# Ten of eleven pairs of the down projection through seven block products, in five groups of two

## The chip, the cores and the metric

The kernel runs on one core of one Trainium2 chip. The metric is the device time of one launch in microseconds (us), the median of several runs. TensorE multiplies matrices into PSUM (8 banks of 128x512 float32), VectorE and ScalarE read PSUM and work on SBUF, SyncE issues the DMAs between the chip's main memory and SBUF. Every instruction of an engine runs in the order in which it was issued to that engine.

## The reference

One encoder layer with a final norm, applied to 1024 + 256 = 1280 tokens of width 1024 (two request groups, the same weights), float32:

```
h = x + 0.5 * swiglu(rmsnorm(x, g1), gate1, up1, down1)
u = rmsnorm(h, gm) @ w_in            # queries, keys, values, retention, gate
h = h + concat(windowed_attention(u), silu(u_gate) * retention(u)) @ w_out
h = h + 0.5 * swiglu(rmsnorm(h, g2), gate2, up2, down2)
y = rmsnorm(h, g_final)
swiglu(x, G, U, D) = (silu(x @ G) * (x @ U)) @ D      # 1024 -> 2816 -> 1024
```

The change lies in the last product, `@ D`, of both feed-forwards.

## The kernel before

Tokens lie along the free dimension, in chunks `CH`: chunks 0 and 1 of 512 tokens, chunk 2 of 256. A tile is 128 features by one chunk. The 2816 inner features are 22 tiles; tile t and tile t + 11 (`HALF` = 11) form pair t, so there are eleven pairs, 0 to 10. Every float32 operand is split into a high and a low fp32r half (`split`, line 517: a cast on ScalarE, a subtraction on VectorE), and every product is three matmuls, high x high, high x low, low x high (`part`, line 535).

A feed-forward (`ffn`, line 663) has two parts. In the first, gate and up, each pair t goes through `product` twice (two "units" of about 25 us); `finish(t)` (line 781) splits its activations and stores them to main memory as tiles `a`. In the second, down, the tiles come back (`act`, line 793, tiles `xa`), and the result `h` (24 tiles: 8 row tiles by 3 chunks) is summed over the pairs.

Down multiplies a 2x2 block matrix (two tiles of a pair by two halves of the 8 row tiles) with a 2x2 block of activations (two tiles of a pair by chunks 0 and 1). `down(ts)` (line 823) does this for the pairs in `ts` with the seven products of Strassen's scheme (Winograd's form): for each of four m, seven products over 512 tokens instead of eight, plus four products for chunk 2's 256 tokens. `seven` (line 628) makes the weight combinations, `combos` (line 618) those of the activations, as operands 6, 7, 5 and 4; operands 1, 2, 3 are tiles as they are, 8 and 9 those of chunk 2. Weights are loaded in two halves `mh`, each for two m. Each finished bank is added into `h` by `add` (line 826): the first addition to a tile is a copy on ScalarE, all later ones are on VectorE. After the second, third and fourth group the residual is loaded and added (lines 898 to 903).

`down_last(ts)` (line 801) does the last two pairs directly, chunk by chunk, so that each chunk is finished in turn and the norm behind it (`after`, a generator) can start: in the first feed-forward `finish1(0)` (line 929), which norms and splits chunk 0 for the input projection, in the second `norm_out` (line 649), which writes the output. Chunk 1's norm in the first feed-forward follows at line 1296, then `factors` (line 919) makes the combinations of both chunks for the products of `joint` (line 1076).

Nothing of this is issued as written. `Weaver` (line 100) records all operations and orders them for each engine by list scheduling with costs and due times (`arrange`, line 269), within the number of buffers: 104 SBUF tiles of 128x512 (`s2`, line 479) are shared by activations, weights, their splits and `h`. A load may be issued up to 300 operations ahead of TensorE's front and must leave 6 tiles free. All DMAs are issued by SyncE in one order. Since all instructions are emitted by one line, every row of the profile bears line 445; groups are told apart by tile names: `pa` and `pb` are PSUM banks (gate/up, and down), `raw` loaded weights, `w`, `wh`, `wl` their halves, `xa` loaded activations, `a` stored ones.

The first group's activations are loaded early, in the last product of gate/up (`early`, line 886).

Of the kernel before, what the change touches and what calls it, by code (L numbers as in the profile page):

```python
# [457 lines left out]
def tile_encoder_layer(ctx: ExitStack, tc: tile.TileContext, xT, wf1, w_in, w_out, wf2,  # L458
# [11 lines left out]
    def nm(s):  # L470
        cnt[0] += 1
        return f"{s}_{cnt[0]}"
# [22 lines left out]
    def bank_b():  # L495
        return nc.tile(psp, [P, 512], F32, "p", nm("pb"), 8, True)
# [7 lines left out]
    cols = nc.tile(cpool, [P, 8], F32, None, "cols", 1)  # L504
# [12 lines left out]
    def split(src, dt_tile_hi, dt_tile_lo):  # L517
        nc.scalar.copy(dt_tile_hi, src)
        nc.vector.tensor_tensor(dt_tile_lo, src, dt_tile_hi.bitcast(F32), op=ALU.subtract)

    def fetch(src, W=512):

        t = big(W, name="raw")
        nc.sync.dma_start(t, src)
        return t

    def halves(t, W=512, together=False):
        hi, lo = two(W, "w", together)
        split(t, hi, lo)
        return hi, lo  # L530

    def unit(src):
        return [halves(fetch(src[:, i * 512:(i + 1) * 512])) for i in range(2)]

    def part(ps, w, x, W, start, stop, cols=None):


        n = 3 * len(x)
        i = 0
        for k, (xh, xl) in enumerate(x):  # L540
            ws = cols if cols is not None else slice(k * P, (k + 1) * P)
            nc.bundle()
            for a, b in ((w[0], xh), (w[0], xl), (w[1], xh)):
                nc.tensor.matmul(ps[:, :W], lhsT=a[:, ws], rhs=b[:, :W], start=start and i == 0,
                                 stop=stop and i == n - 1, skip_group_check=True)
                i += 1
            nc.unbundle()
# [65 lines left out]
    def pair(t, W):  # L613
        a, b = two(W, "x")
        split(t[:, :W], a[:, :W], b[:, :W])
        return a, b

    def combos(b11, b12, b21, b22):


        t1, n2, t3, t4 = (s2(name=n) for n in ("t1", "n2", "t3", "t4"))
        nc.vector.tensor_tensor(t1, b11, b12, op=ALU.subtract)
        nc.vector.scalar_tensor_tensor(n2, t1, -1.0, b22, op0=ALU.mult, op1=ALU.subtract)
        nc.vector.tensor_tensor(t3, b22, b12, op=ALU.subtract)
        nc.vector.scalar_tensor_tensor(t4, n2, -1.0, b21, op0=ALU.mult, op1=ALU.subtract)
        return {i: pair(t, 512) for i, t in ((6, n2), (7, t3), (5, t1), (4, t4))}
# [36 lines left out]
    def ffn(tag, wsrc, leads, factors, load, after, direct_pairs):  # L663
# [4 lines left out]
        HALF = NFF // 2  # L668
# [112 lines left out]
        def finish(t, acts):  # L781
            a11, a12, a21, a22, a1, a2 = acts
            ops = {1: pair(a11, 512), 2: pair(a21, 512), 3: pair(a22, 512),
                   **(combos(a11, a12, a21, a22) if t < HALF - 2 else {10: pair(a12, 512)}),
                   8: pair(a1, 256), 9: pair(a2, 256)}
            for i, p in ops.items():
                keep[t, i] = []
                for n, b in enumerate([p[0].buf] if p[0].buf is p[1].buf else [s.buf for s in p]):
                    d = nc.tile(dp, [P, 512], F32, None, f"a{tag}_{t}_{i}_{n}", 1)
                    nc.sync.dma_start(d, View(b).bitcast(F32))  # L790
                    keep[t, i].append(d)

        def act(t, i):
            out = []
            for d in keep[t, i]:
                s = s2(F32R, "xa")
                nc.sync.dma_start(s.bitcast(F32), d)
                out.append(s)
            return out if len(out) == 2 else (out[0][:, :256], out[0][:, 256:512])

        def down_last(ts, h):
            ws = [unit(wsrc[u, :, 2, :]) for t in ts for u in (t, t + HALF)]
            closing = iter(())
            for c, parts in enumerate(((1, 2), (10, 3), (8, 9))):
                xa = [act(t, i) for t in ts for i in parts]
                W = CH[c][1]
                for d in range(KT):
                    ps = bank_b()
                    for i, (w, x) in enumerate(zip(ws, xa)):
                        part(ps, w[d // 4], [x], W, i == 0, i == len(ws) - 1, slice(d % 4 * P, (d % 4 + 1) * P))  # L810
                    nc.vector.scalar_tensor_tensor(h[c][d][:, :W], ps[:, :W], 0.5, h[c][d][:, :W],
                                                   op0=ALU.mult, op1=ALU.add)

                    if d >= 4:
                        next(closing, None)
                before, closing = closing, iter(after(c))
                next(closing, None)
                for _ in before:
                    pass
            for _ in closing:  # L820
                pass

        def down(ts, h, xa=None):
            xa = xa or {i: [act(t, i) for t in ts] for i in (1, 2, 6, 7, 5, 4, 3, 8, 9)}

            def add(c, d, ps, sign):
                W = CH[c][1]
                if h[c][d] is None:
                    h[c][d] = big(W, name="h")
                    nc.scalar.activation(h[c][d][:, :W], ps[:, :W], AF.Copy, scale=0.5 * sign)  # L830
                else:
                    nc.vector.scalar_tensor_tensor(h[c][d][:, :W], ps[:, :W], 0.5 * sign, h[c][d][:, :W],
                                                   op0=ALU.mult, op1=ALU.add)

            for mh in range(2):
                ws = []
                for t in ts:
                    r = []
                    for u in (t, t + HALF):
                        x = s2(name="raw")  # L840
                        src = wsrc[u, :, 2, :].rearrange("p (i c) -> p i c", i=2)
                        nc.sync.dma_start(x.rearrange("p (i c) -> p i c", i=2), src[:, :, mh * 256:mh * 256 + 256])
                        r.append([x[:, i * 256:i * 256 + 256] for i in range(2)])
                    ws.append(dict(seven(r[0][0], r[1][0], r[0][1], r[1][1], 256)))
                for mm in range(2):
                    m = 2 * mh + mm
                    cols = slice(mm * P, mm * P + P)

                    def all_(ps, i, x, W, start, stop):
                        n = len(ts) - 1  # L850
                        for k, w in enumerate(ws):
                            part(ps, w[i], [xa[x][k]], W, start and k == 0, stop and k == n, cols)

                    X, Y, Z = bank_b(), bank_b(), bank_b()
                    d1, d2 = bank_b(), bank_b()
                    all_(X, 1, 1, 512, True, True)
                    add(0, m, X, 1)
                    all_(d1, 1, 8, 256, True, False)
                    all_(Z, 2, 2, 512, True, True)
                    add(0, m, Z, 1)  # L860
                    all_(d1, 2, 9, 256, False, True)
                    add(2, m, d1, 1)
                    all_(X, 6, 6, 512, False, True)
                    add(0, m + 4, X, -1)
                    all_(Y, 7, 7, 512, True, True)
                    add(1, m + 4, Y, -1)
                    all_(X, 5, 5, 512, False, True)
                    add(1, m + 4, X, -1)
                    all_(Y, 4, 4, 512, False, True)
                    add(0, m + 4, Y, -1)  # L870
                    all_(d2, 4, 9, 256, True, False)
                    all_(X, 3, 3, 512, False, True)
                    add(1, m, X, 1)
                    all_(d2, 21, 8, 256, False, True)
                    add(2, m + 4, d2, 1)

        last = next(leads)
        finish(0, direct(0, last))
# [5 lines left out]
        first = {}  # L884

        def early(i):
            if i == 2:
                first.update({j: [act(0, j)] for j in (1, 2, 6, 7, 5, 4, 3, 8, 9)})

        for t in range(direct_pairs, HALF):  # L890
            finish(t, seven_eighths(t, t == direct_pairs, *[early] * (t == HALF - 1)))
        for c in range(3):
            h[c] = [None] * KT
        groups = [[0], [1, 2], [3, 4], [5, 6], [7, 8]]
        for n, g in enumerate(groups):
            down(g, h, first if n == 0 else None)

            if 1 <= n <= 3:
                c = n - 1
                W = CH[c][1]  # L900
                for d in range(KT):
                    t = load(c, d)
                    nc.vector.tensor_tensor(h[c][d][:, :W], h[c][d][:, :W], t[:, :W], op=ALU.add)
        down_last([9, 10], h)


    h = {c: [None] * KT for c in range(3)}
# [386 lines left out]
    for c in pr:  # L1294
        if c == 1:
            finish1(1)
        ps = [bank_a(), bank_a()]
# [22 lines left out]
    for name, ld, col in (("wf", LDF, 0), ("wb", LDB, 1), ("cf", LDF, 4), ("cb", LDB, 4)):  # L1320
        t = nc.tile(cpool, [P, 4], F32, None, name, 1)
# [177 lines left out]
```

## Time and profile before

| | |
|---|---|
| runs | 2270.89, 2273.5, 2271.23 us; median 2271.23 |
| profiled execution | 2270.64 us, of which the span from first to last instruction 2268.7 |
| mean granted clock of TensorE | 0.995 of 2.4 GHz |
| busy: TensorE | 2236.5 us (99%) |
| busy: VectorE | 1646.5 us (73%) |
| busy: ScalarE | 982.7 us (43%) |
| moved by DMA | 340.06 MB, mean 150 GB/s |

A record of a matmul is longer than its share of the engine, because matmuls overlap; what the engine spends on one is the distance between starts. The number of matmuls is that of the instructions of TensorE. A wait is put down to the instruction that came last before it ended.

### The profile page before, as it was taken

What the parts mean: (1) busy time and instruction counts of PE and PEld (TensorE: products, weight loads), DVE (VectorE), ACT (ScalarE), POOL (GpSimd) and SP (SyncE); (2) the same over time, 40 slices, a digit from 0 to 9 for tenths busy, and PEclk for the clock granted to TensorE, in tenths of its full rate; (3) what the DMA queues carried; (4) which work ended last, traced back from release to release, by engine and by line L of the source; (5) the groups of instructions that cost most, each with busy time, mean ns of one, the idle gap of its engine ahead of it and who ended that gap; (6) DMA issues with size and microseconds to landing.
All of it is one profiled execution on the core that took longest, in us unless ns stands there. A gap on an engine that the chain in (4) does not pass through costs nothing.

```text
span 2268.7 us, 34074 instructions
## 1 busy us (share of the span) xinstructions
PE 2236.5 (99%) x12234; PEld 1916.9 (84%) x12234; DVE 1646.5 (73%) x3259; ACT 982.7 (43%) x2058; POOL 27.7 (1%) x31
## 2 busy tenths in 40 slices
PE   9999999999999999999999999999999999999998
PEld 8788888888888888888788778888888888888887
DVE  8966666665778769986888886586656666487856
ACT  7533444334422235344788574354433444432311
POOL 0000000000000000000000100000000000000000
PEclk9999999999999999999999999999999999999999
DMA  4333343335776633335533353143333334857722
GB/s 169 126 116 128 137 158 108 121 112 192 277 247 231 216 114 98 116 103 173 186 103 93 128 180 107 50 160 130 112 116 112 130 131 145 281 200 267 254 74 93
DMA packets 198601, 340.06 MB, mean 150 GB/s; under 512 B 21280, under 2 KB 45728, under 8 KB 198432
## 3 DMA queue, kind: packets, MB, share of 16 engines
q1 hardware_dynamic: 198432, 337.89, 43.4%
q8 instruction: 96, 1.57, 0.3%
q14 instruction: 73, 0.60, 0.1%
HBM read 225.61 MB, written 112.20 MB: 149 GB/s over the span
## 4 chain that ended last, share of the span: by engine, by line
PE 89%; DMA 5%; DVE 3%; ACT 1%; issue 1%; SPq 0%; POOL 0%; POOLq 0%; DVEq 0%; ACTq 0%
PE pa L445 62%; PE pb L445 25%; DMA raw<-wf 2%; PE pc L445 1%; DMA xa<-a 1%; DMA h<-xT 1%; DVE h L445 1%; DVE xl L445 1%; DMA h<-hf 0%; DVE s L445 0%; ACT sq L445 0%; DVE wl L445 0%; SPq L445 0%; DVE w L445 0%; DVE t L445 0%
## 5 line engine op out<-in xcount | busy, mean ns | idle before, releaser
L445 PE MATMUL pa<-xh,wh 128*128 128x512 f32 x1624 | 637.3, 392 | 3.2 <-ACT xh L445 2.7
L445 PE MATMUL pa<-xl,wh 128*128 128x512 f32 x1624 | 634.4, 391 | 1.3 <-DVE xl L445 1.3
L445 PE MATMUL pa<-xh,wl 128*128 128x512 f32 x1624 | 632.8, 390 | 0.0
L445 PE MATMUL pb<-xa,w 128*128 128x512 f32 (+1 forms) x2376 | 454.2, 353 | 6.5 <-ACT h L445 4.5
L445 PEld LDWEIGHTS pb<-xa,w 128*128 128x128 f32 x2376 | 387.4, 189 | 73.4 <-ACT h L445 5.7
L445 PEld LDWEIGHTS pa<-xh,wh 128*128 128x128 f32 x1624 | 305.9, 188 | 66.1 <-ACT xh L445 3.6
L445 PEld LDWEIGHTS pa<-xh,wl 128*128 128x128 f32 x1624 | 305.3, 188 | 64.8
L445 PEld LDWEIGHTS pa<-xl,wh 128*128 128x128 f32 x1624 | 306.0, 188 | 59.9 <-DVE xl L445 1.9
L445 PE MATMUL pa<-x,wh 128*128 128x256 f32 x1824 | 341.0, 286 | 0.6 <-ACT wh L445 0.6
L445 PEld LDWEIGHTS pa<-x,wh 128*128 128x128 f32 x1824 | 292.8, 192 | 13.3 <-issue 1.5
L445 DVE SCALAR_TENSOR_TENSOR h<-pb,h 128x512 f32<-128x512 f32 (+1 forms) x360 | 224.3, 630 | 105.4 <-PE pb L445 103.3
L445 PE MATMUL pa<-x,wl 128*128 128x256 f32 x912 | 258.9, 284 | 0.3 <-DVE wl L445 0.2
L445 DVE TENSOR_TENSOR wl<-raw,wh 128x512 fp32r<-128x512 f32 x318 | 211.0, 687 | 33.8 <-PE pa L445 15.2
L445 ACT CAST wh<-raw 128x512 fp32r<-128x512 f32 x318 | 186.4, 621 | 95.8 <-DMA raw<-w_in 43.0
L445 DVE TENSOR_TENSOR o<-o,pa 128x512 f32<-128x512 f32 x150 | 102.3, 684 | 137.9 <-PE pa L445 125.9
L445 ACT ACTIVATE o<-pa 128x512 f32<-128x512 f32 (+1 forms) x109 | 64.4, 591 | 267.5 <-PE pa L445 263.6
L445 PEld LDWEIGHTS pa<-x,wl 128*128 128x128 f32 x912 | 175.0, 192 | 0.9 <-DVE wl L445 0.9
L445 DVE TENSOR_TENSOR wl<-s,wh 128x512 fp32r<-128x512 f32 x200 | 134.1, 688 | 30.9 <-PE pa L445 20.8
L445 ACT CAST wh<-s 128x512 fp32r<-128x512 f32 x200 | 118.6, 619 | 47.5 <-PE pa L445 24.5
L445 ACT ACTIVATE sq<-h 128x512 f32<-128x512 f32 (+1 forms) x96 | 51.0, 557 | 152.8 <-DVE h L445 151.0
L445 ACT CAST w<-raw 128x256 fp32r<-128x256 f32 x144 | 53.2, 404 | 147.0 <-DMA raw<-wf 95.0
L445 DVE TENSOR_TENSOR xl<-s,xh 128x512 fp32r<-128x512 f32 x70 | 48.4, 692 | 88.1 <-ACT xh L445 85.7
(157 smaller groups left out, 2449.2 us busy)
## 6 DMA issues: line engine op xcount, KB each, us to landing
xa<-a SPq DMA_DIRECT2D x328, 256.0 KB, 5.1
raw<-wf SPq DMA_DIRECT2D x264, 256.0 KB, 5.0
a<-xh SPq DMA_DIRECT2D x142, 256.0 KB, 2.1
a<-xl SPq DMA_DIRECT2D x142, 256.0 KB, 3.4
raw<-w_in SPq DMA_DIRECT2D x88, 256.0 KB, 3.6
o<-o SPq DMA_DIRECT2D x80, 256.0 KB, 2.8
raw<-w_out SPq DMA_DIRECT2D x48, 256.0 KB, 3.4
a<-x SPq DMA_DIRECT2D x44, 256.0 KB, 2.3
```

What stands on the lines that cost most here:

```text
L445: i = getattr(getattr(self.nc, eng), method)(*[r(x) for x in a], **{m: r(x) for m, x in k.items()})
```

## The change

The groups of `down` become [0, 1], [2, 3], [4, 5], [6, 7], [8, 9] instead of [0], [1, 2], [3, 4], [5, 6], [7, 8]; `down_last` does pair 10 alone for chunks 0 and 1, and pairs 10 and 9 for chunk 2. So chunk 2 of pair 9 (`HALF - 2`) is left out of the group [8, 9]. `early` loads the tiles of pairs 0 and 1. `finish(9)` now stores the combinations instead of operand 10. The diff, with repeated guards of the same kind left out:

```
@@ finish
-                   **(combos(a11, a12, a21, a22) if t < HALF - 2 else {10: pair(a12, 512)}),
+                   **(combos(a11, a12, a21, a22) if t < HALF - 1 else {10: pair(a12, 512)}),
@@ down_last
-        def down_last(ts, h):
-            ws = [unit(wsrc[u, :, 2, :]) for t in ts for u in (t, t + HALF)]
+        def down_last(h):
+            ws = [unit(wsrc[u, :, 2, :]) for u in (HALF - 1, 2 * HALF - 1)]
             closing = iter(())
             for c, parts in enumerate(((1, 2), (10, 3), (8, 9))):
-                xa = [act(t, i) for t in ts for i in parts]
+                if c == 2:
+                    ws = ws + [unit(wsrc[u, :, 2, :]) for u in (HALF - 2, 2 * HALF - 2)]
+                xa = [act(t, i) for t in ((HALF - 1,), (HALF - 1,), (HALF - 1, HALF - 2))[c] for i in parts]
@@ down
-            xa = xa or {i: [act(t, i) for t in ts] for i in (1, 2, 6, 7, 5, 4, 3, 8, 9)}
+            t2 = [t for t in ts if t != HALF - 2]
+            xa = xa or {i: [act(t, i) for t in (ts if i < 8 else t2)] for i in (1, 2, 6, 7, 5, 4, 3, 8, 9)}
...
                     def all_(ps, i, x, W, start, stop):
-                        n = len(ts) - 1
-                        for k, w in enumerate(ws):
-                            part(ps, w[i], [xa[x][k]], W, start and k == 0, stop and k == n, cols)
+                        n = len(xa[x]) - 1
+                        for k, a in enumerate(xa[x]):
+                            part(ps, ws[ts.index(t2[k]) if W == 256 else k][i], [a], W, start and k == 0,
+                                 stop and k == n, cols)
...
-                    all_(d1, 1, 8, 256, True, False)
+                    if t2:
+                        all_(d1, 1, 8, 256, True, False)
...
@@ ffn
-                first.update({j: [act(0, j)] for j in (1, 2, 6, 7, 5, 4, 3, 8, 9)})
+                first.update({j: [act(t, j) for t in (0, 1)] for j in (1, 2, 6, 7, 5, 4, 3, 8, 9)})
...
-        groups = [[0], [1, 2], [3, 4], [5, 6], [7, 8]]
+        groups = [[0, 1], [2, 3], [4, 5], [6, 7], [8, 9]]
...
-        down_last([9, 10], h)
+        down_last(h)
```

## Rows read from the trace of the kernel before

**Rows 1.** The page, part 1: busy us (share of the span) and instructions of each engine.

```profile
PE 2236.5 (99%) x12234; PEld 1916.9 (84%) x12234; DVE 1646.5 (73%) x3259; ACT 982.7 (43%) x2058; POOL 27.7 (1%) x31
```

**Rows 2.** Groups of instructions by form: count, busy us and mean ns, idle before.

```profile
L445 PE MATMUL pb<-xa,w 128*128 128x512 f32 x1512 | 377.4, 394 | 6.5 <-ACT h L445 4.5 <-DVE h L445 2.0
...
L445 DVE TENSOR_TENSOR w<-raw,w 128x256 fp32r<-128x256 f32 x144 | 58.6, 418 | 3.0 <-ACT w L445 2.8
...
L445 ACT CAST w<-raw 128x256 fp32r<-128x256 f32 x144 | 53.2, 404 | 147.0 <-DMA raw<-wf 95.0 <-PE pb L445 41.1 <-DVE h L445 9.0
...
L445 DVE TENSOR_TENSOR xl<-s,xh 128x512 fp32r<-128x512 f32 x70 | 48.4, 692 | 88.1 <-ACT xh L445 85.7 <-PE pa L445 1.2 <-ACT s L445 0.8
```

**Rows 3.** Timeline of TensorE in down_last: start us, us, engine, form, count.

```profile
2236.37 0.39 PE L445 MATMUL pb<-xa,wl 128*128 128x512 f32 x1
...
2243.85 0.39 PE L445 MATMUL pb<-xa,wl 128*128 128x512 f32 x1
```

**Rows 4.** Instructions on tile `pb`, 560 to 880 and 1960 to 2270 us.

```profile
L445 PE MATMUL pb<-xa,w x1188: 274/389/500, 574.2 to 804.0; 128*128 128x512 f32 x126, 128*128 128x256 f32 x72
...
L445 PE MATMUL pb<-xa,w x1188: 274/389/628, 1968.2 to 2198.6; 128*128 128x512 f32 x125, 128*128 128x256 f32 x73
```

**Rows 5.** Busy us by engine in two stretches, clock, DMA share, GB/s.

```profile
core 0: us, PE busy (x) PEld busy (x) DVE busy (x) ACT busy (x) POOL busy (x), PEclk, DMA share, GB/s
574.20:599.00 24.80, 22.91 (x120) 19.17 (x119) 14.77 (x34) 14.85 (x33) 0.00 (x0) 1.00 1.05 380
1968.20:1995.00 26.80, 24.24 (x120) 20.37 (x120) 14.23 (x31) 14.14 (x32) 0.00 (x0) 0.94 1.03 373
```

**Rows 6.** TensorE's waits in 560:620, 1960:2020, 640:690, 740:780, 2030:2075 (2130:2165 alike).

```profile
PE pb L445 <- ACT h L445: 1.9, 2, 1.2
...
PE pb L445 <- ACT h L445: 2.6, 1, 2.6
...
PE pb L445 <- DVE h L445: 1.4, 2, 0.9
...
PE pb L445 <- DVE h L445: 0.3, 1, 0.3
...
PE pb L445 <- DVE h L445: 0.2, 1, 0.2
```

**Rows 7.** The chain of waits at the second entry: start us, us, what.

```profile
1974.21 6.03 DMA a<-x
...
1980.30 5.13 DMA raw<-wf
...
1985.45 0.71 ACT w L445 x2
...
1986.74 0.51 ACT h L445
```

**Rows 8.** Timeline of the DMA issues, second feed-forward: start, us, count.

```profile
1921.42 18.65 SPq L445 DMA_DIRECT2D xa<-a  x14
```

**Rows 9.** DMA issues from 1957 to 1998 us: count, KB each, us to landing.

```profile
xa<-a SPq DMA_DIRECT2D x35, 256.0 KB, 5.4
```

**Rows 10.** Busy us by engine in five stretches, as rows 5.

```profile
1921.00:1940.00 19.00, 19.00 (x105) 16.55 (x104) 7.28 (x12) 4.18 (x8) 0.00 (x0) 1.00 0.62 193
754.00:804.00 50.00, 49.74 (x263) 42.33 (x262) 36.25 (x70) 10.23 (x21) 0.00 (x0) 1.00 0.44 154
804.00:829.00 25.00, 25.00 (x115) 20.77 (x114) 11.14 (x17) 5.07 (x9) 0.00 (x0) 1.00 0.32 109
829.00:980.00 151.00, 151.00 (x731) 127.36 (x731) 141.18 (x244) 72.49 (x128) 2.25 (x2) 1.00 0.35 117
980.00:1080.00 100.00, 100.00 (x461) 82.97 (x459) 68.33 (x122) 50.53 (x97) 0.00 (x0) 1.00 0.42 138
```

**Rows 11.** Timelines of VectorE and ScalarE around one joint product.

```profile
953.83 0.68 DVE L445 TENSOR_TENSOR wl<-raw,wh 128x512 fp32r<-128x512 f32 x1
...
964.90 0.58 ACT L445 COPY o<-pa 128x512 f32<-128x512 f32 x1
```

**Rows 12.** Busy us by engine at the end of the kernel, as rows 5.

```profile
2198.60:2260.00 61.40, 59.47 (x326) 51.65 (x325) 37.72 (x65) 13.46 (x24) 2.13 (x2) 1.00 0.16 62
```

More of the change, by code (lines that the diff above doesn't have):

```diff
@@ L849, in all_ @@
                     def all_(ps, i, x, W, start, stop):
-                        n = len(ts) - 1
-                        for k, w in enumerate(ws):
-                            part(ps, w[i], [xa[x][k]], W, start and k == 0, stop and k == n, cols)
+                        n = len(xa[x]) - 1
+                        for k, a in enumerate(xa[x]):
+                            part(ps, ws[ts.index(t2[k]) if W == 256 else k][i], [a], W, start and k == 0,
+                                 stop and k == n, cols)
                     X, Y, Z = bank_b(), bank_b(), bank_b()
-                    d1, d2 = bank_b(), bank_b()
+                    if t2:
+                        d1, d2 = bank_b(), bank_b()
                     all_(X, 1, 1, 512, True, True)
                     add(0, m, X, 1)
-                    all_(d1, 1, 8, 256, True, False)
+                    if t2:
+                        all_(d1, 1, 8, 256, True, False)
                     all_(Z, 2, 2, 512, True, True)
                     add(0, m, Z, 1)
-                    all_(d1, 2, 9, 256, False, True)
-                    add(2, m, d1, 1)
+                    if t2:
+                        all_(d1, 2, 9, 256, False, True)
+                    if t2:
+                        add(2, m, d1, 1)
                     all_(X, 6, 6, 512, False, True)
@@ L870, in down @@
                     add(0, m + 4, Y, -1)
-                    all_(d2, 4, 9, 256, True, False)
+                    if t2:
+                        all_(d2, 4, 9, 256, True, False)
                     all_(X, 3, 3, 512, False, True)
                     add(1, m, X, 1)
-                    all_(d2, 21, 8, 256, False, True)
-                    add(2, m + 4, d2, 1)
+                    if t2:
+                        all_(d2, 21, 8, 256, False, True)
+                    if t2:
+                        add(2, m + 4, d2, 1)
         last = next(leads)
```

## The prediction

> **What bounds the kernel now.** I read the engines' shares first. TensorE has a matmul running for 2236.5 of 2268.7 us, so whatever shortens the span must take matmuls away or remove one of its few waits [rows 1]. The groups of instructions then give the work of the stage that changes: the matmuls into `pb` from `xa`, 128x512 and 128x256, and the small VectorE and ScalarE instructions that prepare their weights [rows 2]. The distance between two starts, not the 394 ns of a record, is what a matmul costs: eleven triples of 128x512 start from 2236.37 to 2243.85 us, 7.48/33 = 0.2267 us each [rows 3].
>
> The products of the second matrix ("down") run from 574.2 to 804.0 us in the first feed-forward and from 1968.2 to 2198.6 us in the second [rows 4]. TensorE waits at three kinds of places around them. At the entry, while the single pair [0] runs, it stands still for 24.80 - 22.91 = 1.9 us in the first feed-forward and 26.80 - 24.24 = 2.6 us in the second; in the second alone the mean granted clock is 0.94 of 2.4 GHz, so part of it ran at the 1.2 GHz level, around the time when TensorE had stood still [rows 5], and the waits name ScalarE's first-touch copy `h` [rows 6]. The chain says why: a store `a<-x` landed late, the weights `raw<-wf` behind it too, ScalarE stood in order at the cast `w`, and the copy `h` behind that cast released TensorE [rows 7]. The DMA share is 1.03 to 1.05 in these stretches [rows 5]. Between groups of two it waits for VectorE's `h`, 1.4, 0.3 and 0.2 us where it does [rows 6]. After the stage (down_last and what follows) TensorE waits for nothing between 804 and 1080 us, but VectorE is busy for 141.18 of 151 us from 829 to 980 [rows 10]: it is the next bound there.
>
> **The change, part by part.**
>
> *Matmuls.* For pair 9, chunks 0 and 1 cost directly 2 chunks x 8 tiles x 2 units x 3 terms = 96 matmuls of 128x512, by seven products 4 x 7 x 3 = 84. Chunk 2 costs 48 of 128x256 either way, and for pair 9 it stays direct. Twelve go in each feed-forward: 24 x 0.2267 = 5.4 us less [rows 3]. It counts in full since TensorE is what the end waits for. The Trainium skill, page "TensorE: Matmul & The Clock Gate", section "Wait — 56ns, not 53.3ns?", puts back-to-back matmuls of 512 columns at 215.7 ns; by that the term would be an estimated 5.2 us. The rows show 226.7 ns, and I keep theirs.
>
> *Preparing pair 9.* Its activations need `combos`: 4 sums and net 3 more splits, 7 x 0.69 = 4.8 us of VectorE and about 1.9 of ScalarE [rows 2], during the products of pair 10, where VectorE is busy 7.28 of 19 us [rows 10]. Its weights need 24 VectorE instructions of 0.42 us and 16 casts of 0.4 us [rows 2], 10 and 6.5 us, but are also still split directly for chunk 2 as before. They fall in groups [6, 7] and [8, 9]; from 754 to 804 us VectorE has 13.7 us free and ScalarE 39.8 [rows 10]. The number of groups stays five, so the additions into `h` stay 36 per group. DMAs grow by 6 stores, 6 loads of activations and 4 of weights per feed-forward, 256 KB each, spread over stretches with shares of 0.44 to 0.62 [rows 10]. I cost all this at nothing; uncovered it would be at most those 4.8 + 10 us per feed-forward.
>
> *Entry.* Group [0, 1] replaces [0]. Before, TensorE's 24.8 us with one pair had to hide the loads of [1, 2]: 35 activation tiles from 1957 to 1998 us, with 5.4 us from issue to landing [rows 9]. Afterwards [2, 3] has two such stretches. ScalarE's 24 copies and its casts, 14.85 of 24.80 us before [rows 5], spread as well. In exchange 32 tiles must be there within the first quarter of the group (12.4 us). Sixteen come in before the last product starts, 14 of them from 1921 to 1940 us [rows 8]; in the burst that follows before, another 35 arrive that then belong to [1, 2], and the same burst would bring the missing 16. The stalls to be won are 1.9 + 2.6 us, and the slower clock: 230.4 us for the second feed-forward's stage [rows 4] less its waits of 2.6 + 0.2 + 0.2, against 229.8 less 1.9 + 1.4 + 0.3, is 1.2 us more. Together 5.7. The bounds are 0 left and, if the tiles come late, more than before (rival C). I take 0.75 left in each, between the 0.2 and the 1.4 of a boundary between two groups of two, where as many tiles arrive [rows 6]: 4.2 us less. The new boundary [0, 1] to [2, 3] costs like the other six, (1.4 + 0.3 + 0.2 + 0.2)/6 = 0.35 each (0 to 1.4), 0.7 us more.
>
> *Exit, first feed-forward.* down_last loses 96 matmuls of chunks 0 and 1, 21.8 us of cover (they stand in group [8, 9] instead, 84 of them), while VectorE's work behind it stays: additions into `h`, squares, norms, splits of the next inputs and weights. From 804 to 980 us that is 11.14 + 141.18 = 152.3 us [rows 10], in 176 us before and 154.2 after. At VectorE's rate of 829 to 980 us, 93.5%, it takes 162.9: it falls 8.7 us behind. Against that stands its lead: the weights of a joint product are split at 954.5, and its first 12 matmuls (2.7 us) end when ScalarE copies the result at 964.9 [rows 11], so they start at about 962: 7.5 us of lead. After 980 VectorE is busy 68%, so the lag does not grow. I take 1.5 us lost; bounds 0 (no gaps: 152.3 < 154.2) and 8.7 (no lead is usable). What is late next is the norm of chunk 1 and the combinations of the normed input.
>
> *Exit, second feed-forward.* VectorE does 37.72 us from 2198.6 to 2260.0 [rows 12]; 61.4 - 21.8 = 39.6 are left, and at 93.5% it needs 40.3: 0.7 us later at the end. Bounds: 0, and 12.4 if VectorE works only at the 72.5% of 754 to 804 us [rows 10]; there it waited for matmuls, here it would be behind them, so I stay at the low end.
>
> *Sum.* -5.4 - 4.2 + 0.7 + 1.5 + 0.7 = -6.7 us on the profiled 2270.64 us (span 2268.70 and 1.9 around it): 2263.9. The median shown is 0.6 above that run: 2264.5.
>
> **Rivals.**
>
> A, the forecast: entry eased, exit mostly covered; 2264.5, own range 2259.5 to 2266.6.
>
> B, the shorter cover at the exit decides: VectorE's lead cannot be used, because those splits already lie as early as room allows. Then 8.7 instead of 1.5 us: 2271.7; with half of it 2268.1. For it speaks VectorE's 93.5% and that nothing else in the kernel is so full; against it the 7.5 us of lead and that its own waits vanish once it is behind. Taken at half, 2268.
>
> C, slower: group [0, 1] starves at its start. Room for its second 16 tiles and the second pair's weights comes only as the last product frees its inputs, and 16 more tiles held early leave less for the weights. If all 32 activation tiles and 4 of weights, with 7 stores among them, begin at 1957 us, where the burst of before begins, 43 tiles of 0.262 MB at about 375 GB/s [rows 5], 0.70 us each, are issued by 1987.4, the last lands 5.4 us later [rows 9] at 1992.8, and the first quarter would end at 1980.6: 12.2 us and the clock's 1.2, twice 13.4 instead of 1.5 in all: 2290. It turns slower than before from about 4.1 us per entry, for without any entry stall the rest saves 8.2. Against it: 16 tiles came in by 1940 [rows 8]. The Trainium skill's "Perfetto Trace Analysis", section "Optimization Strategy", says that repeated bubbles can mean that no room is left for the next tile; the trace shows no repeated gap before 1968.
>
> D, the change does only half of what it could: the 24 matmuls go, but the entry's stalls just move with the first group, since the store that held back the weights [rows 7] is still issued there. Then -5.4 + 0.7 + 1.5 + 0.7 = -2.5: 2268.7. For it speaks that ScalarE's order of casts and copies is unchanged; against it that the weights of the second half are now needed 25 instead of 12 us into the group.
>
> **How the numbers follow.** A 0.62, B 0.14, C 0.09, D 0.15. A change of 0.2% (4.5 us, about what a measurement of this kernel can tell from none) starts at 2266.7. A lies below it, with some mass of B and D: faster 0.64. B and D mostly fall within: same 0.26. C, and B beyond its bound: slower 0.10. The low end of the range takes both entries and exits at 0 (2271.23 - 11.1 = 2260.1) and 1.5 us for waits elsewhere that a new order may remove, 2258.6. The high end is B in full, 2271.7, so that only C is outside: 2272.
>
> **What would show it.** 24 matmuls fewer, all 128x512 (12210 in all). No wait of TensorE over 1 us in the first 25 us of either stage, clock 1.00 there. The DMA share of that stretch falls below 0.9 for [0, 1]. In the first feed-forward VectorE has hardly a gap from the start of down_last for 150 us; TensorE waits of more than 2 us for VectorE there mean B. In the second, the time from the last matmul into `h` to the end grows by under 1.5 us. An entry wait over 4 us is C. The prediction is wrong if TensorE's waits elsewhere change by more than 3 us in all, since I hold them constant.

## The result, and the profile after

The changed kernel takes 2282.39 us (median of 4 runs, 2281.56 to 2283.92) against 2271.39 of the kernel before beside it: ratio 1.0054, 95% interval 1.0043 to 1.0066. It is slower by half a per cent where 0.3% faster was forecast, and it lies above the forecast's range. The profiled execution took 2283.05 us, its span 2281.1, 12.4 more than before.

The page's first part, as [rows 1]:

```profile
PE 2236.4 (98%) x12210; PEld 1915.7 (84%) x12210; DVE 1667.5 (73%) x3321; ACT 997.4 (44%) x2096; POOL 28.2 (1%) x31
```

The 24 matmuls are gone. TensorE's busy time did not fall with them, since more of the others ran at the lower clock: the mean granted clock is 0.992 of 2.4 GHz, where it was 0.995. The instructions on tile `pb` (first and last start after the comma), as [rows 4]; `w` is the grouped down, `wl` belongs to down_last:

```profile
L445 PE MATMUL pb<-xa,w x1272: 274/389/628, 575.4 to 829.8; 128*128 128x512 f32 x120, 128*128 128x256 f32 x62
...
L445 PE MATMUL pb<-xa,wl x64: 283/336/397, 830.4 to 865.0; 128*128 128x512 f32 x32, 128*128 128x256 f32 x32
...
L445 PE MATMUL pb<-xa,w x1272: 277/389/792, 1973.8 to 2232.0; 128*128 128x512 f32 x120, 128*128 128x256 f32 x62
...
L445 PE MATMUL pb<-xa,wl x64: 279/336/397, 2232.5 to 2268.9; 128*128 128x512 f32 x32, 128*128 128x256 f32 x32
```

The same instructions of down_last before:

```profile
L445 PE MATMUL pb<-xa,wl x96: 283/389/397, 804.6 to 861.0; 128*128 128x512 f32 x64, 128*128 128x256 f32 x32
...
L445 PE MATMUL pb<-xa,wl x96: 279/389/397, 2199.1 to 2257.2; 128*128 128x512 f32 x64, 128*128 128x256 f32 x32
```

This gives the account of the 12.4 us. Grouped down went from 229.8 to 254.4 us in the first feed-forward and from 230.4 to 258.2 in the second, +24.6 and +27.8. The 84 matmuls that moved in account for 84 x 0.2267 = 19.0 of each [rows 3]; so 5.6 and 8.8 us are loss. Down_last, from the last start on `w` to the last on `wl`, went from 57.0 to 35.2 and from 58.6 to 36.9, -21.8 and -21.7, as worked out beforehand. The start of the first down moved by +1.2, what lies between the two by +1.6, the tail by +0.7 (differences of starts, to 0.2 us).

TensorE's waits from 575 to 640 us and from 1973 to 2050 us (us in total, times, longest), as the first two lines of [rows 6], say where the loss sits:

```profile
PE pb L445 <- ACT h L445: 3.4, 2, 2.2
PE pb L445 <- DVE h L445: 1.9, 1, 1.9
...
PE pb L445 <- DVE h L445: 6.1, 1, 6.1
PE pb L445 <- ACT h L445: 2.9, 2, 1.8
```

That is 5.3 and 9.0 us at the two entries, where it was 1.9 and 2.6: 3.4 and 6.4 of the 5.6 and 8.8. The rest goes with a lower clock and with the waits between the groups; no run separates them. Three stretches of the second entry (us, busy us by engine in the order of [rows 5], granted clock, DMA share, GB/s):

```profile
1980.00:1990.00 10.00, 5.99 (x28) 4.53 (x27) 4.46 (x12) 2.49 (x6) 0.00 (x0) 1.00 1.05 395
1990.00:2000.00 10.00, 6.13 (x25) 5.31 (x26) 4.97 (x13) 2.48 (x6) 0.00 (x0) 0.66 0.48 173
2000.00:2010.00 10.00, 10.00 (x53) 8.53 (x53) 9.21 (x24) 6.09 (x17) 0.00 (x0) 1.00 0.00 0
```

The reader sees three things. TensorE stands still for 4 of 10 us in each of the first two. In the second its mean clock is 0.66 of 2.4 GHz, so most of that stretch ran at the 1.2 GHz level; with the standstill, 25 matmuls started in 10 us, half of the 53 in the next 10. And VectorE and ScalarE are no busier than TensorE while the DMA engines are full at 1.05; these then fall to nothing, 0.00: the transfers were not too many for the stage. That they came in the wrong order is what the experiments have to show.

SyncE's issues around the second entry, as [rows 8] (start, us, count). Down starts at 1973.8:

```profile
1957.78 2.34 SPq L445 DMA_DIRECT2D raw<-wf  x4
1960.43 0.34 SPq L445 DMA_DIRECT2D a<-xh  x1
...
1965.26 1.64 SPq L445 DMA_DIRECT2D xa<-a  x3
...
1972.28 3.66 SPq L445 DMA_DIRECT2D xa<-a  x6
1976.28 0.32 SPq L445 DMA_DIRECT2D a<-xh  x1
...
1983.52 2.90 SPq L445 DMA_DIRECT2D xa<-a  x5
1987.66 0.32 SPq L445 DMA_DIRECT2D a<-xh  x1
1988.29 0.32 SPq L445 DMA_DIRECT2D a<-xl  x1
```

All 32 tiles of [0, 1] had been issued before 1957.78. From 1965.26 on every `xa<-a` is a tile of the next group, [2, 3]: 21 of them and 4 of its weights `raw` stand between the first and the last store of pair 10. The chain of waits over that stretch (start, us, what), as [rows 7]:

```profile
1969.29 6.93 DMA xa<-a
...
1976.28 5.24 DMA a<-xh
...
1981.59 6.01 DMA a<-xl
...
1987.66 5.11 DMA a<-xh
...
1992.79 0.04 DVE s L445
...
1993.14 0.69 DVE h L445
...
1993.87 28.26 PE pb L445 x138
```

Landing, issue, landing, issue: 5 to 7 us each. At its end stands VectorE (timelines of VectorE, then of TensorE; in brackets the idle time before and what ended it):

```profile
1981.55 0.42 DVE L445 TENSOR_TENSOR s<-raw,raw 128x256 f32<-128x256 f32 x1 [1.77 <-DMA a<-xh]
...
1992.79 0.42 DVE L445 TENSOR_TENSOR s<-raw,raw 128x256 f32<-128x256 f32 x1 [6.75 <-DMA a<-xh]
1993.14 0.68 DVE L445 SCALAR_TENSOR_TENSOR h<-pb,h 128x512 f32<-128x512 f32 x1
...
1984.75 3.03 PE L445 MATMUL pb<-xa,w 128*128 128x512 f32 x12 [1.79 <-ACT h L445]
1993.87 18.36 PE L445 MATMUL pb<-xa,w 128*128 128x512 f32 x88 [6.10 <-DVE h L445]
```

VectorE's instructions at 1981.55 and 1992.79 are weight sums `s`, for the second half of [0, 1]. Their inputs are there, since all weights of [0, 1] were issued by 1965; they wait for a store, that is for the room that the store's tile gives up. The addition into `h`, which TensorE needs in order to have a bank free, stands behind the second in VectorE's order.

Loads among the stores are nothing new, though. In the kernel before, 29 tiles of its next group [1, 2] stand between the first and the last store of pair 10, at both entries, more than here. There VectorE's sums waited for late loads of weights instead; its only wait for a DMA from 1960 to 2020 us:

```profile
DVE s L445 <- DMA raw<-wf: 4.8, 1, 4.8
```

ScalarE did wait for a store there, 2.7 us; here it is 9.2. What is new is that 32 tiles of the first group are held beside the early loads instead of 16, and that its sums are twice as many. The likely reading is that the queue is as crowded as before and that the room now runs short for the sums too.

The exits cost little. TensorE's waits from 865 to 1060 us and from 2200 us on:

```profile
PE pa L445 <- DVE xl L445: 0.4, 1, 0.4
...
PE pb L445 <- POOL r L445: 1.6, 1, 1.6
```

The wait for `r` was 1.1 us before. What lies between the two downs grew by 1.6 us, of which TensorE's waits there make up 0.5; the rest is not explained.

### The profile page after: what moved, and what is told of

It reads as the page before. It is cut to its first block, busy times and chain, and to the rows that moved or that the text cites. A ratio compares the mean times of both kernels' runs of the same rounds, so it can differ in the third digit from the quotient of the medians.

```text
span 2281.1 us, 34232 instructions
## 1 busy us (share of the span) xinstructions
PE 2236.4 (98%) x12210; PEld 1915.7 (84%) x12210; DVE 1667.5 (73%) x3321; ACT 997.4 (44%) x2096; POOL 28.2 (1%) x31
## 4 chain that ended last, share of the span: by engine, by line
PE 88%; DVE 5%; DMA 4%; ACT 1%; issue 1%; SPq 0%; POOL 0%; DVEq 0%; ACTq 0%; POOLq 0%
PE pa L445 61%; PE pb L445 26%; PE pc L445 1%; DMA raw<-wf 1%; DVE xl L445 1%; DVE h L445 1%; DMA a<-xl 1%; DVE t L445 1%; DMA xa<-a 1%; DVE s L445 1%; DMA h<-xT 1%; DVE wl L445 0%; DMA a<-xh 0%; ACT sq L445 0%; DVE w L445 0%
## 5 line engine op out<-in xcount | busy, mean ns | idle before, releaser
L445 PE MATMUL pb<-xa,w 128*128 128x512 f32 (+1 forms) x2544 | 496.1, 357 | 17.0 <-DVE h L445 10.6
L445 PEld LDWEIGHTS pb<-xa,w 128*128 128x128 f32 x2544 | 421.2, 190 | 92.0 <-DVE h L445 14.8
L445 DVE TENSOR_TENSOR wl<-s,wh 128x512 fp32r<-128x512 f32 x200 | 133.9, 687 | 35.2 <-PE pa L445 23.3
L445 ACT CAST w<-raw 128x256 fp32r<-128x256 f32 x160 | 58.2, 404 | 155.5 <-PE pb L445 71.4
L445 ACT CAST w<-s 128x256 fp32r<-128x256 f32 x160 | 62.7, 405 | 118.1 <-DVE s L445 93.8
```

Of the source, the lines that this page charges most:

```text
L445: i = getattr(getattr(self.nc, eng), method)(*[r(x) for x in a], **{m: r(x) for m, x in k.items()})
```

## The experiments

Times are medians of 2 to 11 runs, ratios are to the kernel before on the same chip. The theories, as the expectations call them: **S**, pair 10's stores stand behind loads for [2, 3] in SyncE's queue, which take the room; in form S1 the order does it, in S2 the room in whatever order. **W** puts it on what [0, 1] asks for itself, early. **B** on the DMA engines' bandwidth alone. **L**, later, on the time a store needs to land.

| kernel | tiles of the next group among pair 10's stores (1st, 2nd) | entry waits, us | median, us | ratio, 95% interval |
|---|---|---|---|---|
| before | 29, 29 | 1.9, 2.6 | 2271.39 | 1 |
| e8_before_stores_first | 0, 0 | none | 2273.52 | 1.0016 (1.0007 to 1.0025) |
| changed | 22, 21 | 5.3, 9.0 | 2282.39 | 1.0054 (1.0043 to 1.0066) |
| e7_room100 | 18, 18 | 6.1, 5.6 | 2286.88 | 1.0075 (1.0056 to 1.0095) |
| e4_late1 | 13, 13 | 4.6, 4.5 | 2277.10 | 1.0024 (1.0015 to 1.0034) |
| e6_ahead200 | 6, 4 | 2.7, 2.5 | 2302.87 | 1.0146 (1.0132 to 1.0160) |
| e5_stores_first | 0, 0 | 1.3, 0.6 | 2266.02 | 0.9982 (0.9973 to 0.9991) |
| e1_gate | 0, 0 | 0.4, 0 | 2264.76 | 0.9971 (0.9962 to 0.9980) |
| e10_gate_all | 0, 0 | 0.8, 0 | 2266.60 | 0.9983 (0.9974 to 0.9992) |
| e9_copies | 0, 0 | 0.8, 0 | 2280.12 | 1.0041 (1.0028 to 1.0053) |
| e2_pool | stores in another queue | 4.1, 3.5 | 2276.36 | 1.0024 (1.0015 to 1.0033) |
| e3_six (single pair first) | 29, 29 | 1.4, 1.6 | 2265.04 | 0.9980 (0.9969 to 0.9990) |

The tiles are counted in SyncE's order of issue, the waits are TensorE's near each entry. e6, e7, e8 and e9 lose time elsewhere as well, told below. The first two rows and e3 begin the stage with one pair, all others with two. The number of tiles alone does not set the waits: 29 with one pair cost less than 13 with two. But with either grouping the waits nearly go once no tile stands among the stores.

**e1_gate: the loads of [2, 3] wait their turn.** In the planner, a load of [2, 3] may be placed only when TensorE's front has reached the second half of [0, 1]:

```
-            if op.eng == "SP" and op.idx > front() + self.AHEAD:
+            if op.eng == "SP" and (op.idx > front() + self.AHEAD or op.gate > front()):
...
+            nc.gate = half[0] if n == 1 else 0
             down(g, h, first if n == 0 else None)
```

> The loads for the second group [2, 3] (32 activation tiles, 4 of weights) may be issued only when TensorE has reached the second half of group [0, 1]. Theory S (room and one queue: the stores of pair 10 stand in SyncE's order behind loads for [2, 3] that wait for room, and VectorE's weight sums wait for the tiles which those stores hold): the entry waits of 5.3 and 9.0 us fall to under 1.5 us each and the clock stays at 1.00, so 2282.4 becomes 2266 to 2270. Theory B (too many bytes in that stretch for the DMA engines): also faster, as the stretch has fewer bytes, 2266 to 2272. Theory W (32 tiles loaded early make the first weights late): unchanged, 2281 to 2283.

Measured: 2264.76 us, 6.4 below the kernel before beside it and 17.6 below the changed one. That is 1.2 us below the ranges of S and B, which both expected a gain; W, which expected none, falls. SyncE's issues at the second entry (down starts at 1966.3 here):

```profile
1968.93 0.32 SPq L447 DMA_DIRECT2D a<-xh  x1
1969.66 0.32 SPq L447 DMA_DIRECT2D a<-xl  x1
...
1976.77 13.49 SPq L447 DMA_DIRECT2D xa<-a  x19
```

The last store goes out 3.4 us after the start of down instead of 14.5, and the burst of loads stands behind it. Two stretches of 10 us there:

```profile
1970.00:1980.00 10.00, 9.91 (x50) 7.84 (x50) 9.46 (x26) 5.22 (x13) 0.00 (x0) 1.00 0.98 341
1980.00:1990.00 10.00, 10.00 (x54) 8.61 (x53) 2.39 (x5) 2.29 (x5) 0.00 (x0) 1.00 1.06 390
```

The DMA engines are as full as before, 0.98 and 1.06, the clock is 1.00 and TensorE's gaps sum to 0.09 us. So a full set of DMA engines does not by itself cost anything here, once the stores are out; e9 below has them full beside the stores as well, with entry waits of 0.8 and 0 us. B falls. The same data, a few microseconds later, are free.

**e2_pool: pair 10's stores on GpSimd's queue.**

```
-                    nc.sync.dma_start(d, View(b).bitcast(F32))
+                    (nc.gpsimd if t == HALF - 1 else nc.sync).dma_start(d, View(b).bitcast(F32))
```

> Only the ten stores of pair 10 in each feed-forward go through GpSimd's DMA queue instead of SyncE's; bytes and prefetch stay. Theory S: the stores no longer stand behind loads, the tiles come free earlier; the waits fall to about half or less (from 5.3 + 9.0 to under 6 in all), 2268 to 2276. Theory B: the same bytes on the same DMA engines, unchanged within 2 us, 2280 to 2284. Theory W: unchanged.

Measured: 2276.36, just above S's range. The entry waits fall from 14.3 to 7.6 us, about half, where S expected under 6; the time falls by 6.0 us, a third of what e1 gained. The chain at the second entry ends so:

```profile
1973.19 6.25 DMA a<-xl
...
1979.53 0.61 ACT h L445
...
1980.18 35.03 PE pb L445 x166
```

A place in another queue lets a store start, but the loads of [2, 3] still come early, and a store lands 6.25 us after its issue. Queueing behind the loads was about half of the waits. Whether the other half is the shared DMA engines or the room that the loads hold, this run does not say; e9 bears on it.

**e3_six: the arithmetic without the new entry.** Groups [0], [1, 2], ... [7, 8], [9]: pair 9 goes through seven products, but the stage begins with one pair as before.

```
-                first.update({j: [act(t, j) for t in (0, 1)] for j in (1, 2, 6, 7, 5, 4, 3, 8, 9)})
+                first.update({j: [act(0, j)] for j in (1, 2, 6, 7, 5, 4, 3, 8, 9)})
...
-        groups = [[0, 1], [2, 3], [4, 5], [6, 7], [8, 9]]
+        groups = [[0], [1, 2], [3, 4], [5, 6], [7, 8], [9]]
```

> Groups [0], [1, 2], [3, 4], [5, 6], [7, 8], [9]: the entry with one pair as before the change, the same 24 matmuls fewer, 28 more additions into h on VectorE (19 us, beside TensorE). If the loss is all at the entry (S, B and W alike): entry waits of 1.9 and 2.6 us as before, about 2266 to 2270. If the shorter direct tail or the preparation of pair 9 costs, it stays above 2274.

Measured: 2265.04, 1.0 below the range and 6.2 below the kernel before, with 12210 matmuls. Part of that is the entry: its waits are 1.4 and 1.6 us instead of 1.9 and 2.6, and the clock at the second is 1.00 instead of 0.94. In the first feed-forward, where the clock was 1.00 before too, down and down_last together take 283.5 us instead of 286.8; that is the 2.7 of twelve matmuls and the 0.5 of the wait, to 0.2 us. So the matmul term is there in full, and preparing pair 9 costs nothing that can be seen. What lies between the two downs is 0.9 us longer than before and the tail 0.8, so the exits do cost a little. The loss of the change comes with its first group of two pairs.

**e4_late1: half as many tiles early.** Only pair 0's 16 tiles are asked for in the last product.

```
-                first.update({j: [act(t, j) for t in (0, 1)] for j in (1, 2, 6, 7, 5, 4, 3, 8, 9)})
+                first.update({j: [act(0, j)] for j in (1, 2, 6, 7, 5, 4, 3, 8, 9)})
...
-            down(g, h, first if n == 0 else None)
+            down(g, h, {j: a + [act(1, j)] for j, a in first.items()} if n == 0 else None)
```

> As after, but in the last product only the 16 tiles of pair 0 are asked for; those of pair 1 are asked for with the group. Theory W: the first weights come earlier and the entry waits fall by half or more, 2270 to 2276. Theory S: 16 tiles of room are free longer but the same loads and stores share the queue; little change, 2279 to 2284, or slower since pair 1's tiles can come late. Theory B: as S.

Measured: 2277.10, between the two ranges. Both were wrong: it is better than S had it and worse than W had it, with waits of 4.6 and 4.5 us. Two things changed at once: 13 instead of 21 tiles of [2, 3] now stand among the stores (8 of [0, 1]'s own take the place of the others), and fewer tiles of pair 1 are held early. The run does not say which of the two made it better.

**e5_stores_first and e8_before_stores_first: the order alone, after and before.** Every load for the second group gets the stores of pair 10 as predecessors in the plan; the reach and the room stay. The same edit goes into the kernel before.

```
+            nc.behind = tuple(stores) if n == 1 else ()
             down(g, h, first if n == 0 else None)
...
+        if op.eng == "SP":
+            op.deps.update(self.behind)
```

> In SyncE's order the loads for group [2, 3] follow right behind the last store of pair 10 instead of lying among the stores; nothing else holds them back. Theory S1 (order: what costs is that stores stand behind loads which wait for room): entry waits under 1.5 us each, 2264 to 2268, as with the loads held to the second half. Rival S2 (room: the early loads of [2, 3] take the tiles which VectorE's weight sums need, in whatever order): the waits stay above 3 us each, 2272 to 2280.

> The kernel before with the same order: its loads for [1, 2] behind the last store of pair 10. S1: its entry waits of 1.9 and 2.6 us and the slower clock there have the same cause and shrink to under 1 us each, 2266 to 2269, unless the loads of [1, 2], needed 25 us after the start, now come late. S2: unchanged or slower, 2270 to 2276.

Measured: 2266.02 and 2273.52 (1.0016, 1.0007 to 1.0025). In the changed kernel the order brings 16.4 us back, so S1 holds and S2, in whatever order, falls. Room is not ruled out as the means, since loads behind the stores also take it later: at the second entry they start 4.5 us after down instead of 8.5 before it. In the kernel before, S1 expected a gain unless the loads of [1, 2] came late. It costs 3.0 us against the kernel before beside it, which is inside S2's range, but the trace shows S1's exception. Its trace at the second entry (SyncE's issues, then TensorE):

```profile
1979.70 18.29 SPq L448 DMA_DIRECT2D xa<-a  x26
1998.36 4.40 SPq L448 DMA_DIRECT2D raw<-wf  x7
...
2004.29 5.91 PE L448 MATMUL pb<-xa,w 128*128 128x512 f32 x22 [2.18 <-ACT w L448]
```

The entry itself has no wait left, but [0] alone lasts about 25 us, and 26 tiles and 7 weights issued behind the stores are not all in by then: TensorE waits 2.4 and 2.2 us for the weights `w` of [1, 2]. The order is worth what the first group is long enough to hide.

**e6_ahead200 and e7_room100: reach and room.**

```
-    AHEAD = 300
+    AHEAD = 200
```

```
-    NS2, NS1 = 104, 12
+    NS2, NS1 = 100, 12
```

> After with one number changed: loads may be issued 200 instead of 300 operations ahead of TensorE's front, everywhere. It puts only three loads of [2, 3] ahead of the last store of pair 10. S1: 2264 to 2270. S2: also better, since the room is filled later, 2266 to 2272. If a bound elsewhere needs the longer reach, above 2272 with waits outside the entries.

> After with 100 instead of 104 shared SBUF tiles. S2 (room): the entry waits grow by several us, 2286 to 2295. S1 (order): as many loads as in after still stand among the stores, so the waits stay about as they are, 2279 to 2286.

Measured: 2302.87 and 2286.88. e6 came out as its third case had it and says little on time, since the shorter reach holds for the whole kernel; TensorE's waits in its first 200 us contain

```profile
PE pa L445 <- DVE wl L445: 21.5, 3, 21.0
```

where the kernels before and after have 0.2. At its entries, though, 6 and 4 tiles of [2, 3] are left among the stores, and the waits are 2.7 and 2.5 us. e7 has only two runs, 2284.75 and 2289.01, one in S1's range and one in S2's; its entry waits sum to 11.7 us, less than the changed kernel's 14.3, and part of the rest was lost at the boundaries between groups (waits for VectorE's `h` away from the entries, 5.7 us against 2.6). With four tiles fewer, room is short in more than one place, so it does not separate the theories; e5 does.

**e9_copies: full DMA engines without the room.** e1 with one thing added: once the first store of pair 10 has landed, GpSimd's queue copies it 24 times within main memory. SyncE's order is that of e1.

```
+        nc.bundle()
+        for n in range(24):
+            nc.gpsimd.dma_start(nc.tile(dp, [P, 512], F32, None, f"b{tag}_{n}", 1), keep[HALF - 1, 1][0])
+        nc.unbundle()
```

> The gated kernel (loads for [2, 3] behind the stores of pair 10) with one thing added: as soon as the first store of pair 10 has landed, GpSimd's own queue copies that stored tile 24 times from main memory to main memory, 256 KB each, as many as there are loads of [2, 3] among the stores in the changed kernel. The copies take no SBUF room and do not stand in SyncE's queue; they only share the 16 DMA engines with the stores. The copies are work that the reference does not need. Theory S1 (what costs in the changed kernel is the place in SyncE's queue and the room that the loads wait for): nothing comes back, the entries keep waits under 1 us each, 2264 to 2267. Theory L (what costs is that a store lands 5 us after its issue instead of 2 when other transfers share the DMA engines, so room comes late and VectorE and ScalarE stand in order): the stores land after 4 us or more, waits of 2 to 4 us return at each entry, as when the stores had their own queue, 2270 to 2276. If both act, the time lies between and the landing time of the stores says how much of it is L.

Measured: 2280.12, beyond both ranges. The time looks like L, the trace does not. Median us from issue to landing of the stores issued from 1955 to 2000 us (count, size, us), in the changed kernel:

```profile
a<-xh SPq DMA_DIRECT2D x4, 256.0 KB, 5.2
```

in e1:

```profile
a<-xh SPq DMA_DIRECT2D x3, 256.0 KB, 2.0
```

and in e9:

```profile
a<-xh SPq DMA_DIRECT2D x4, 256.0 KB, 9.0
a<-xl SPq DMA_DIRECT2D x4, 256.0 KB, 10.5
```

The stores land later than in the changed kernel, and TensorE still waits only 0.8 and 0 us at the entries. It waits 45 us after the start of down, at the boundary to [2, 3], 5.0 us in the first feed-forward and 4.2 in the second (its timeline; SyncE's issue of the weights before it):

```profile
2012.92 2.57 SPq L447 DMA_DIRECT2D raw<-wf  x4
...
2023.74 6.52 PE L447 MATMUL pb<-xa,w 128*128 128x512 f32 x19 [4.24 <-ACT h L447]
```

The copies pushed the loads of [2, 3] back; VectorE stood in order at the sums of weights that came late, the copy `h` behind them; the clock fell around that wait (0.66 from 2020 to 2030 us). So a slow landing alone does not stall the entry as long as nothing else takes the room meanwhile: L by itself falls as the cause of the entry's waits. Together with e2 this leaves, for the half of the waits that a queue of their own did not cure, the room that the early loads hold, and the trace after shows VectorE waiting for just that. Still, that step is by elimination; no run varied the room alone at this place without touching the order.

**e10_gate_all: the gate for every group** (the edit is against e1).

```
-                if ts[0] == 0 and mh == 1:
+                if mh == 1:
                     half.append(len(nc.ops))
...
-            nc.gate = half[0] if n == 1 else 0
+            nc.gate = half[-1] if n else 0
```

> The gate for all groups: the loads of each group may be issued only when TensorE's place in the plan is in the second half of the group before. The first kernel with the gate had it for [2, 3] alone: 2264.8, and its waits at the four boundaries were 1.4 and 0.8 us per feed-forward. At these boundaries no stores are under way, so the theory of the stores says that nothing is to be won: 2263.5 to 2266. The rival, that any early load is harmful since it takes room from the weight sums of the current group, says the boundary waits go too, up to 2.2 us in all: 2261 to 2263.5. If loads now come too late, waits for weights appear at the boundaries and it is over 2266.

Measured: 2266.60, 0.6 above the first range, with boundary waits of 1.5 and 0.5 us against 1.4 and 0.8 in e1. Nothing is won at boundaries without stores, so the rival falls; the waits for weights that would explain a time over 2266 are not there either. The intervals of e10 and e1 overlap, so the 1.8 us between them mean nothing.

The best versions are e1_gate (2264.76) and e3_six (2265.04); both beat both kernels, and the runs don't tell them apart.

## Why the prediction was wrong, step by step

*Matmuls, -5.4.* Right. 24 fewer, down_last 21.8 and 21.7 us shorter, and in the first feed-forward of e3 the twelve matmuls' 2.7 us are found beside the 0.5 of the wait.

*Preparing pair 9 at nothing.* Right by e3.

*Exits, +1.5 and +0.7.* The second was right, the tail grows by 0.7. After the first TensorE waits 0.4 us for `xl` behind VectorE, so the mechanism is there, and smaller than forecast; the stretch up to the second down grows by 1.6 all the same (1.1 in e1, 0.9 in e3), mostly not as a wait, so that the number fits partly by luck. Rival B, at 0.14, is not seen.

*New boundary, +0.7.* Right: the waits at all boundaries are 1.5 + 1.1 us against 1.7 + 0.3.

*Entry, -4.2.* This step failed, at the sentence "I take 0.75 left in each". Measured: 5.3 and 9.0 us of waits, where 1.9 and 2.6 had been, and over the first 24.8 us a mean clock of 0.93 and 0.86, where 1.00 and 0.94 (over 26.8 us) had been. The stretches, as [rows 5]:

```profile
575.40:600.20 24.80, 19.57 (x94) 16.06 (x93) 18.40 (x48) 10.12 (x27) 0.00 (x0) 0.93 0.85 317
1973.80:1998.60 24.80, 15.81 (x71) 12.86 (x70) 14.91 (x40) 7.74 (x19) 0.00 (x0) 0.86 0.86 312
```

Its premise was "Afterwards [2, 3] has two such stretches": that the loads would spread over the longer first group. They did not. The planner issues a load as soon as it is within 300 operations of TensorE's front and 6 tiles are free, not when it is needed; so 21 tiles of [2, 3] came in the old place, between pair 10's stores, where 29 of [1, 2] had been, while the first group held 16 tiles more; and in the second half of the group the queue was idle (share 0.00 from 2000 to 2010). I asked how much the DMA engines had to carry in the stretch and not who stands behind whom, although [rows 7] already showed a load behind a store. The observable that I named, a share below 0.9 in the first 24.8 us, came true (0.85 and 0.86) and meant nothing: 1.05, then zero.

*Rival C* had the right place, the right sign and the right point of decision (from 4.1 us per entry; measured 5.3 and 9.0), and its remark that 16 more tiles held early leave less room for the weights was sound; but what it made late was wrong, and its chance of 0.09 too small. The second 16 tiles and the weights were not late: all had been issued by 1965. What ran out was room for the weight sums of [0, 1], with the next group's tiles in it: in e1 and e5 the first group holds its 32 tiles as early, and the waits nearly go. The 16 tiles that I held against C were true and beside the point.

The Trainium skill's page "Perfetto Trace Analysis", section "Optimization Strategy", says that repeated bubbles on the engine to be kept busy can mean that the next tile finds no room. I had set this aside because the trace of before shows no repeated gap. The trace after shows three gaps in the first 20 us of the second down, of 1.1, 1.8 and 6.1 us, unequal ones; VectorE's instruction that held up the longest waited for the landing that freed room, so here the Trainium skill was the better guide.

The Trainium skill's page "DMA: Bandwidth & Descriptors", section "Anatomy of one DMA — SWDGE (gpsimd) path", gives one DMA on GpSimd's queue a fixed part of about 2.0 us plus its bytes by 436 GB/s; for 256 KB that is an estimated 2.6 us. The stores on that queue (e2) took 5.6 to 6.3 us from issue to landing while the 16 DMA engines were busy for about 0.9 of the stretch, so there the measurement is over twice the Trainium skill's figure. On SyncE's queue, for which the section has no formula, they took 2.0 in e1, 5.2 in the changed kernel and 9.0 in e9.

With the stores first (e1) the change is worth -6.4 us, against the forecast's -6.7. The terms fit there too: the two stages together are 9.2 us shorter, where matmuls, entries and boundary made 8.9, and the rest is 2.8 longer, where the exits made 2.2 (0.9 of the 2.8 lies ahead of the first down, where nothing was forecast). The sum of terms was right for a kernel whose loads come when they are needed; the written change was not that kernel.

## What to carry to other kernels

When a change lengthens the work ahead of a group, ask of every load that it lets go early what it is queued in front of and whose room it takes, above all while the last results of the stage before are still being stored. A mean DMA share says nothing on this: read the issue order of the queue and the landing that each waiting instruction was released by. Putting stores ahead of the next group's loads paid 16 us where the first group was long enough to hide those loads, and cost 3 us where it was not. And the same loads in the same place can be cheap as long as there is room left: 29 tiles among the stores went with 4.5 us of waits in the kernel before, 21 and 22 with 14.3 in the changed one, whose first group holds twice as much.

## What was not expected of the hardware

A 256 KB store took 2.0 us from issue to landing in e1, 5.2 in the changed kernel and 9.0 to 10.5 beside a second queue's 24 copies (e9): a factor of 5 by what else is under way. And the longest stalls of TensorE in this stage went with a stretch at a lower granted clock (0.66 over the 10 us around the end of the 6.1 us wait in the changed kernel, 0.66 around the 4.2 us wait in e9), while e1 kept 1.00 at its entry.
